# Top-10 indices of 8,192 rows: extraction of tile 60 moved behind the last sums, a fourth thin tile, constant matmuls in the last gather, and the rows of one batch on GpSimd

## The chip, the cores and the metric

The kernel runs on one core of one Trainium2 chip. The metric is the device time of one execution in microseconds (us). "Executions" below are single runs of the whole kernel. Every ratio given is the mean time of one kernel's runs over the mean of the kernel before's runs in the same rounds, so it is not quite the ratio of the medians quoted beside it; in the ratios of the experiments the first round, whose execution was profiled, is left out.

## The reference, cut to what matters

```python
# x: 8192 x 8192 float32, k = 10
indices = np.argpartition(x, -k, axis=1)[:, -k:]
values = np.take_along_axis(x, indices, axis=1)
sorted_idx = np.argsort(-values, axis=1)
return np.take_along_axis(indices, sorted_idx, axis=1)      # 8192 x 10 int64
```

For each row the kernel returns the positions of its ten largest values, in falling order.

## The kernel before

The 8,192 rows go through in 64 tiles of 128 rows, numbered 0 to 63. A tile passes through these stations:

1. **load**: the input arrives in chunks by DMA.
2. **weigh**: ScalarE writes exp(36(x - 4.7)) into one of three `e` buffers; TensorE sums groups of it ("sums", bf16 matmuls of 512 columns).
3. **choose**: VectorE finds the 12 groups with the largest sums and writes their index.
4. **gather**: GpSimd fetches those groups from the tile.
5. **spread**: VectorE (and GpSimd, for one half) multiplies by a mask.
6. **extract**: TensorE turns the masked groups into rows of candidates. E60 to E63 name the extractions of the last four tiles, 24 matmul records each.
7. **rank**: VectorE sorts out the ten best.
8. **finish**: per batch of tiles, one-hot steps, rows and a few matmuls make the output.

The last three tiles (`TAIL = 3`) have a "thin" layout, in which choosing is shorter. The part of the schedule that the change touches:

```python
epool = ctx.enter_context(tc.tile_pool(name="e", bufs=3))
...
    for t in range(last):                       # last = 63
        interleave(choose_steps(t), rank_steps(t - LAG) if t >= LAG else [])
        if t >= 1:
            spread(t - 1)
        gather(t)
        weigh(t + 1)
        if 1 <= t < last - 1:
            extract(t - 1)                      # so E60 is queued ahead of ...
        ...
    run(rank_steps(last - 3))
    run(choose_steps(last))
    spread(last - 1)
    gather(last)
    extract(last - 2)
    extract(last - 1)
    ...
    run(rank_steps(last - 2))
    steps = finish_steps(batch_of[last - 3])
    run(steps[:2])
    spread(last, G)
    run(steps[2:7])
    extract(last)
    run(steps[7:-2])
    run(rank_steps(last - 1))
    run(rank_steps(last))
    ...
```

In the loop's last turn (t = 62), `weigh(63)` comes ahead of `extract(61)`. In the turn before it, `extract(60)` follows `weigh(62)`. TensorE therefore has E60 in its queue ahead of the sums of tile 63, and E61 behind them.

Of the kernel before, what the change touches and what calls it, by code (L numbers as in the profile page):

```python
# [10 lines left out]
P = 128  # L11
N = 8192
BANK = 512
KMAX = 10
G = 12
TB = 8
# [3 lines left out]
FINITE = 1e37  # L20
BIG_NEG = -1e30
LAG = 3
TAIL = 3
PAD = 208



# [8 lines left out]
def kernel(  # L36
# [6 lines left out]
    nc = tc.nc  # L43
# [3 lines left out]
    ntiles = nrows // P  # L47

    fp32 = mybir.dt.float32
# [11 lines left out]
    wide, thin = Layout(8), Layout(16)  # L61
# [5 lines left out]

    pad = ctx.enter_context(tc.tile_pool(name="pad", bufs=1)).tile([P, PAD], fp32, name="pad")
    nc.vector.memset(pad[:, 0:1], 0.0)
# [8 lines left out]
    fpsum = ctx.enter_context(  # L78
        tc.tile_pool(name="fpsum", bufs=1, space=bass.MemoryType.PSUM)
    )  # L80

    last = ntiles - 1

    starts = list(range(0, ntiles - TB, TB)) + [ntiles - TB - 1, ntiles - TAIL]
    sizes = [b - a for a, b in zip(starts, starts[1:] + [ntiles])]
    batch_of = {t: b for b, t0 in enumerate(starts) for t in range(t0, t0 + sizes[b])}

# [3 lines left out]
    def layout(t):  # L91
        return thin if t >= ntiles - TAIL else wide

# [26 lines left out]
    nc.vector.memset(ones, 1.0)  # L120
    for lay, nsend in ((wide, TB), (thin, TAIL)):
        R, A, S = lay.R, lay.A, lay.S
# [105 lines left out]
    def extract(t):  # L228
        mk = masked.pop(t)
        gs[t] = gpsum.tile([P, G * thin.R], fp32, tag="g", name="g")  # L230
        R = layout(t).R
        for c in range(G):
            nc.tensor.matmul(gs[t][:, c * R:(c + 1) * R], lhsT=mk[:, c, :, :].rearrange("p a s -> p (a s)"),  # L233
                             rhs=layout(t).place, start=True, stop=True)

    def rank_steps(t):
        n = G * layout(t).R
        g = gs.pop(t)[:, 0:n]
        b = batch_of[t]
        pos = batch[b][1][:, t - starts[b], :]  # L240
        t8a = small.tile([P, 8], fp32, tag="t8a", name="t8a")
        t8b = small.tile([P, 8], fp32, tag="t8b", name="t8b")
        g2 = small.tile([P, G * thin.R], fp32, tag="g2", name="g2")[:, 0:n]
        return [
            lambda: nc.vector.max(out=t8a, in_=g),  # L245
            lambda: nc.vector.match_replace(out=g2, in_to_replace=t8a, in_values=g,  # L246
                                            imm_value=BIG_NEG),
            lambda: nc.vector.max_index(out=pos[:, 0:8], in_max=t8a, in_values=g),  # L248
            lambda: nc.vector.max(out=t8b, in_=g2),  # L249
            lambda: nc.vector.max_index(out=pos[:, 8:16], in_max=t8b, in_values=g2),  # L250
            lambda: nc.vector.tensor_copy(out=tall[:, t:t + 1],
                                          in_=t8b[:, KMAX - 9:KMAX - 8]),
        ]


    def finish_steps(b):
        cidb, posb = batch.pop(b)
        n = sizes[b]
        lay = layout(starts[b])
        R, A, S, W = lay.R, lay.A, lay.S, lay.W  # L260
        r0 = starts[b] * S
        out_rows = out_u32.rearrange("(r a) n -> r (a n)", a=A)

        queue = nc.sync if b >= len(starts) - 2 else nc.scalar
        slot = bpool.tile([P, TB, KMAX], u16, tag="slot", name="slot")[:, 0:n, :]
        low = bpool.tile([P, TB, KMAX], u16, tag="low", name="low")[:, 0:n, :]
        hot = bpool.tile([P, TB, KMAX, G], fp16, tag="hot", name="hot")[:, 0:n]
        pick = bpool.tile([P, TB, KMAX], fp32, tag="pick", name="pick")[:, 0:n, :]
        val = bpool.tile([P, TB, KMAX], fp32, tag="val", name="val")[:, 0:n, :]
        rows = bpool.tile([P, TB, wide.A, KMAX], fp32, tag="rows", name="rows")[:, 0:n, 0:A]  # L270
        if b == len(starts) - 1:
            fo = spsum.tile([P, wide.W], fp32, tag="s", name="fo")
        else:
            fo = fpsum.tile([P, wide.A * KMAX], fp32, tag="fo", name="fo")
        fo = fo[0:n * S, 0:A * KMAX]
        o = opacks[b % 2][0:n * S, 0:A]
        hshape = [P, n, KMAX, G]
        rshape = [P, n, A, KMAX]

        def move(i):  # L280
            nc.tensor.matmul(fo, lhsT=lay.send[:, i, 0:n * S],  # L281
                             rhs=rows[:, i].rearrange("p a k -> p (a k)"),
                             start=i == 0, stop=i == n - 1)

        return [
            lambda: nc.vector.tensor_scalar(
                out=slot, in0=posb[:, 0:n, 0:KMAX], scalar1=R.bit_length() - 1,
                scalar2=None, op0=ALU.logical_shift_right),
            lambda: nc.vector.tensor_scalar(
                out=low, in0=posb[:, 0:n, 0:KMAX], scalar1=R - 1,  # L290
                scalar2=None, op0=ALU.bitwise_and),
            lambda: nc.vector.tensor_tensor(
                out=hot, in0=slot.unsqueeze(3).to_broadcast(hshape),
                in1=slots.unsqueeze(1).unsqueeze(1).to_broadcast(hshape), op=ALU.is_equal),
            lambda: nc.vector.tensor_tensor(
                out=hot, in0=hot, in1=cidb[:, 0:n, 0:G].unsqueeze(2).to_broadcast(hshape),
                op=ALU.mult),
            lambda: nc.vector.reduce_sum(out=pick, in_=hot, axis=X_AX),  # L298
            lambda: nc.vector.scalar_tensor_tensor(
                out=val, in0=low, scalar=float(W), in1=pick, op0=ALU.mult, op1=ALU.add),  # L300
            lambda: nc.vector.tensor_tensor(  # L301
                out=rows, in0=val.unsqueeze(2).to_broadcast(rshape),
                in1=lay.own_a.unsqueeze(1).unsqueeze(3).to_broadcast(rshape), op=ALU.mult),
        ] + [lambda i=i: move(i) for i in range(n)] + [
            lambda: nc.vector.tensor_copy(
                out=o[:, :, :, 0], in_=fo.rearrange("p (a k) -> p a k", k=KMAX)),
            lambda: queue.dma_start(out=out_rows[r0:r0 + n * S, :],
                                        in_=o.rearrange("p a k two -> p (a k two)")),
        ]

    def interleave(*lists):
        for group_ in zip(*[l for l in lists if l]):
# [3 lines left out]
    def run(steps):  # L316
        for step in steps:
            step()
# [3 lines left out]
    with tc.manual_schedule():  # L322
        weigh(0)
        later = []
        for t in range(last):
            interleave(choose_steps(t), rank_steps(t - LAG) if t >= LAG else [])
            if t >= 1:
                spread(t - 1)
            gather(t)
            weigh(t + 1)  # L330
            if 1 <= t < last - 1:
                extract(t - 1)
            todo = {last - 5: 6, last - 4: TB, last - 3: TB}.get(t, 3)
            run(later[:todo])
            later = later[todo:]
            done = t - LAG
            if done >= 0 and batch_of[done] != batch_of[done + 1]:
                later += finish_steps(batch_of[done])
            if t + 3 < ntiles:
                load(t + 3)  # L340
        run(rank_steps(last - 3))
        run(choose_steps(last))
        spread(last - 1)
        gather(last)
        extract(last - 2)
        extract(last - 1)
        nc.vector.tensor_scalar(
            out=good[:, 0:nsums], in0=eall, scalar1=FINITE, scalar2=None, op0=ALU.is_lt,
        )
        run(rank_steps(last - 2))  # L350
        steps = finish_steps(batch_of[last - 3])
        run(steps[:2])
        spread(last, G)
        run(steps[2:7])
        extract(last)
        run(steps[7:-2])
        run(rank_steps(last - 1))
        run(rank_steps(last))


        nc.scalar.activation(out=e10, in_=tall, func=ACTF.Exp, bias=bias[:, 0:1], scale=BETA)
        final = finish_steps(batch_of[last])
        run(final[:-2])
        run(steps[-2:])
        run(final[-2:])
        nc.vector.scalar_tensor_tensor(
            out=good[:, nsums:nsums + ntiles], in0=e10, scalar=SLACK, in1=wall[:, :, G],
            op0=ALU.mult, op1=ALU.is_gt,
        )

    ngood1 = small.tile([P, 1], fp32, tag="ngood1")
    nc.vector.reduce_sum(out=ngood1, in_=good, axis=X_AX)
    gps = fpsum.tile([P, wide.A * KMAX], fp32, tag="fo", name="gps")[0:1, 0:1]
    nc.tensor.matmul(gps, lhsT=ngood1, rhs=ones, start=True, stop=True)
    ngood = consts.tile([1, 1], i32)
    nc.vector.tensor_copy(out=ngood, in_=gps)
# [56 lines left out]
```

## Time and profile before

| what | value |
|---|---|
| timed executions | 683.30, 683.42, 683.85 us |
| span of the profiled execution | 684.6 us |
| last chunk of input landed | 652.0 us |
| last sums end | 658.86 us |
| index of tile 63 written | 662.73 us |
| its gather ends | 667.96 us |
| ranking of tile 63 starts | 675.29 us |

The last five rows are times in the profiled execution, counted from its start. They form one chain: each row waits for the row above. Everything up to the landing is one long stage at the speed of the loads; the change works on the 32 us behind it. The lines themselves stand in the prediction.

### The profile page before, as it was taken

What the parts mean: (1) busy time and instruction counts of PE and PEld (TensorE: products, weight loads), DVE (VectorE), ACT (ScalarE), POOL (GpSimd) and SP (SyncE); (2) the same over time, 40 slices, a digit from 0 to 9 for tenths busy, and PEclk for the clock granted to TensorE, in tenths of its full rate; (3) what the DMA queues carried; (4) which work ended last, traced back from release to release, by engine and by line L of the source; (5) the groups of instructions that cost most, each with busy time, mean ns of one, the idle gap of its engine ahead of it and who ended that gap; (6) DMA issues with size and microseconds to landing.
All of it is one profiled execution on the core that took longest, in us unless ns stands there. A gap on an engine that the chain in (4) does not pass through costs nothing.

```text
span 684.6 us, 7943 instructions
## 1 busy us (share of the span) xinstructions
PE 550.9 (80%) x2645; PEld 345.7 (51%) x2690; DVE 554.9 (81%) x1335; ACT 488.8 (71%) x264; POOL 178.8 (26%) x134
## 2 busy tenths in 40 slices
PE   1588887888888898778887779888978779888786
PEld 0146653554544565545454356455545446656465
DVE  2568888889868987888887995898978798699567
ACT  4777777776877767877777777777777777777820
POOL 0113313313322322321332232232233133223310
PEclk9856788858876678787888885876789778779765
DMA  9999999999999999999999999999999999999800
GB/s 352 420 421 420 419 421 419 421 419 420 420 421 420 419 421 420 421 419 421 420 421 418 420 420 420 420 420 421 419 421 419 421 415 419 418 418 387 323 2 7
DMA packets 73696, 269.77 MB, mean 394 GB/s; under 512 B 4382, under 2 KB 5046, under 8 KB 73654
## 3 DMA queue, kind: packets, MB, share of 16 engines
q1 hardware_dynamic: 72960, 268.54, 96.1%
q10 hardware_dynamic: 694, 0.71, 0.4%
q8 instruction: 21, 0.34, 0.2%
q14 instruction: 21, 0.17, 0.1%
HBM read 268.58 MB, written 0.66 MB: 393 GB/s over the span
## 4 chain that ended last, share of the span: by engine, by line
DMA 63%; PE 8%; DVE 8%; SPq 6%; ACT 6%; issue 4%; POOL 3%; ACTq 0%; DVEq 0%
DMA xt<-in_x_dram 63%; PE s L169 7%; SPq L101 6%; ACT e L162 6%; POOL cand L203 3%; DVE wall L189 2%; PE g L233 1%; DVE m L190 1%; DVE masked L221 1%; DVE cidb L194 0%; DVE cidb L192 0%; DVE wall L193 0%; DVE rows L301 0%; DVE g L246 0%; DVE pick L298 0%
## 5 line engine op out<-in xcount | busy, mean ns | idle before, releaser
L162 ACT ACTIVATE e<-xt,bias 128x4096 bf16<-128x4096 f32 (+2 forms) x131 | 475.5, 3630 | 160.5 <-DMA xt<-in_x_dram 138.6
L169 PE MATMUL s<-e,group 128*128 128x512 bf16 x979 | 335.3, 498 | 123.9 <-ACT e L162 119.6
L169 PEld LDWEIGHTS <-group 128*128 128x128 bf16 x1024 | 122.3, 123 | 310.9 <-issue 255.3
L233 PEld LDWEIGHTS g<-cpack,masked 128*128 128x128 f32 x1536 | 212.2, 219 | 20.4 <-issue 9.0
L233 PE MATMUL g<-cpack,masked 128*128 128x8 f32 (+1 forms) x1536 | 203.7, 272 | 5.0 <-DVE masked L221 2.5
L203 POOL INDIRECT_COPY cand<-xt,idx 128x192 f32 x64 | 64.8, 1013 | 483.2 <-DMA xt<-in_x_dram 168.2
L189 DVE MAX8 wall<-s 128x8 f32<-128x1024 f32 (+1 forms) x64 | 77.2, 1207 | 119.3 <-PE s L169 113.1
L221 POOL TENSOR_TENSOR masked<-cand,cpack 128x768 f32<-128x768 f32 x63 | 113.1, 1795 | 5.2
L192 DVE FIND_INDEX8 cidb<-wall,s 128x8 uint16<-128x1024 f32 (+1 forms) x64 | 76.9, 1201 | 0.0
L194 DVE FIND_INDEX8 cidb<-wall,m 128x8 uint16<-128x1024 f32 (+1 forms) x64 | 76.7, 1198 | 0.0
L190 DVE MATCH_REPLACE8 m<-wall,s 128x1024 f32<-128x1024 f32 (+1 forms) x64 | 76.2, 1191 | 0.0
L193 DVE MAX8 wall<-m 128x8 f32<-128x1024 f32 (+1 forms) x64 | 75.9, 1186 | 0.0
L221 DVE TENSOR_TENSOR masked<-cand,cpack 128x768 f32<-128x768 f32 x64 | 62.0, 969 | 2.2 <-POOL cand L203 2.2
L281 PE MATMUL fo<-rows,send 128*64 128x160 f32 (+3 forms) x128 | 28.0, 370 | 1.1 <-DVE rows L301 1.1
L162 ACT ACTIVATION_READ_ACCUMULATOR e<-xt,bias 128x1 f32 x131 | 24.4, 186 | 0.0
L281 PEld LDWEIGHTS fo<-rows,send 128*64 128x64 f32 (+2 forms) x128 | 18.5, 162 | 3.5 <-DVE rows L301 1.7
L248 DVE FIND_INDEX8 posb<-t8a,g 128x8 uint16<-128x96 f32 (+1 forms) x64 | 16.9, 264 | 0.0
L250 DVE FIND_INDEX8 posb<-t8b,g 128x8 uint16<-128x96 f32 (+1 forms) x64 | 16.8, 263 | 0.0
L246 DVE MATCH_REPLACE8 g<-t8a,g 128x96 f32<-128x96 f32 (+1 forms) x64 | 16.3, 254 | 0.0
L245 DVE MAX8 t8a<-g 128x8 f32<-128x96 f32 (+1 forms) x64 | 16.2, 254 | 0.0
L249 DVE MAX8 t8b<-g 128x8 f32<-128x96 f32 (+1 forms) x64 | 16.1, 251 | 0.0
L195 DVE TENSOR_SCALAR idx<-cidb,cpack 128x12 uint16<-128x12 uint16 x64 | 14.1, 221 | 0.1
(37 smaller groups left out, 94.0 us busy)
## 6 DMA issues: line engine op xcount, KB each, us to landing
xt<-in_x_dram SPq DMA_DIRECT2D x248, 1024.0 KB, 16.3
xt<-in_x_dram SPq DMA_DIRECT2D x16, 512.0 KB, 9.8
out_dram<-opack ACTq DMA_DIRECT2D x6, 80.0 KB, 5.4
cpack<-topk_cpack ACTq DMA_DIRECT2D x1, 141.0 KB, 3.9
out_dram<-opack ACTq DMA_DIRECT2D x1, 70.0 KB
out_dram<-opack SPq DMA_DIRECT2D x1, 60.0 KB, 2.1
out_dram<-opack SPq DMA_DIRECT2D x1, 30.0 KB, 1.5
```

The costliest lines, as they stand in the source:

```text
L101: nc.sync.dma_start(out=dst[:, s:s + n, :], in_=src[:, s:s + n, :])
L162: nc.scalar.activation(out=e[:, 0:n * W], in_=xts[t][:, s0 * W:(s0 + n) * W], func=ACTF.Exp, bias=bias[:, 0:1], scale=BETA, accum_out=eall ...
L169: nc.tensor.matmul(ss[t][:, j:j + BANK], lhsT=lay.group[:, s0 + i, :], rhs=e[:, i * W + j:i * W + j + BANK], start=s0 + i == 0, stop=s0 + ...
L189: lambda: nc.vector.max(out=w16[:, 0:8], in_=m),
L190: lambda: nc.vector.match_replace(out=m2, in_to_replace=w16[:, 0:8], in_values=m, imm_value=-1.0),
L192: lambda: nc.vector.max_index(out=cid[:, 0:8], in_max=w16[:, 0:8], in_values=m),
L193: lambda: nc.vector.max(out=w16[:, 8:16], in_=m2),
L194: lambda: nc.vector.max_index(out=cid[:, 8:16], in_max=w16[:, 8:16], in_values=m2),
L203: nc.gpsimd.add_instruction(mybir.InstIndirectCopy(name=nc.get_next_instruction_name(), ins=[nc.gpsimd.lower_ap(xts[t]), nc.gpsimd.lower_a ...
L221: eng.tensor_tensor(out=masked[t][:, g0:g1], in0=cand[:, g0:g1].unsqueeze(2).to_broadcast(shape), in1=layout(t).own.rearrange("p (c s) -> ...
L233: nc.tensor.matmul(gs[t][:, c * R:(c + 1) * R], lhsT=mk[:, c, :, :].rearrange("p a s -> p (a s)"), rhs=layout(t).place, start=True, stop=True)
L281: nc.tensor.matmul(fo, lhsT=lay.send[:, i, 0:n * S], rhs=rows[:, i].rearrange("p a k -> p (a k)"), start=i == 0, stop=i == n - 1)
```

## The change

The intent is to take E60 out of the way of the last sums, to let the thin layout start one tile earlier, to keep TensorE's clock up for E63 by matmuls on constants, and to take work from VectorE. The core of the diff:

```diff
-TAIL = 3
+TAIL = 4
+WARM = 12
...
+        spreader = nc.gpsimd if b == len(starts) - 2 else nc.vector
...
-            lambda: nc.vector.tensor_tensor(
+            lambda: spreader.tensor_tensor(
                 out=rows, ...
...
+    def warm(n):
+        idle = fpsum.tile([P, BANK], fp32, tag="fo", name="idle")
+        for i in range(n):
+            nc.tensor.matmul(idle, lhsT=wide.group[:, 0, :],
+                             rhs=wide.group[:, 0:BANK // P, :].rearrange("p s m -> p (s m)"),
+                             start=True, stop=True)
...
-            if 1 <= t < last - 1:
+            if 1 <= t < last - 2:
                 extract(t - 1)
...
-        run(rank_steps(last - 3))
+        extract(last - 3)
+        extract(last - 2)
+        steps = finish_steps(batch_of[last - TAIL])
+        run(steps[:4])
         run(choose_steps(last))
         spread(last - 1)
         gather(last)
-        extract(last - 2)
         extract(last - 1)
+        run(rank_steps(last - 3))
+        run(rank_steps(last - 2))
...
-        run(rank_steps(last - 2))
-        steps = finish_steps(batch_of[last - 3])
-        run(steps[:2])
+        warm(WARM)
         spread(last, G)
-        run(steps[2:7])
         extract(last)
+        run(steps[4:7])
         run(steps[7:-2])
```

Left out here are the batch boundaries that follow from `TAIL`, a PSUM tile made one bank wide, and the padding.

More of the change, by code (lines that the diff above doesn't have):

```diff
@@ L22 @@
 LAG = 3
-TAIL = 3
-PAD = 208
+TAIL = 4
+WARM = 12
+PAD = 224
 class Layout:
@@ L82 @@
     last = ntiles - 1
-    starts = list(range(0, ntiles - TB, TB)) + [ntiles - TB - 1, ntiles - TAIL]
+    starts = list(range(0, ntiles - 2 * TB, TB)) + [ntiles - 2 * TB, ntiles - TB - 2, ntiles - TAIL]
     sizes = [b - a for a, b in zip(starts, starts[1:] + [ntiles])]
@@ L273, in finish_steps @@
         else:
-            fo = fpsum.tile([P, wide.A * KMAX], fp32, tag="fo", name="fo")
+            fo = fpsum.tile([P, BANK], fp32, tag="fo", name="fo")
         fo = fo[0:n * S, 0:A * KMAX]
+        spreader = nc.gpsimd if b == len(starts) - 2 else nc.vector
         o = opacks[b % 2][0:n * S, 0:A]
@@ L330 @@
             weigh(t + 1)
-            if 1 <= t < last - 1:
+            if 1 <= t < last - 2:
                 extract(t - 1)
-            todo = {last - 5: 6, last - 4: TB, last - 3: TB}.get(t, 3)
+            todo = {last - 6: 6, last - 5: TB, last - 4: TB}.get(t, 3)
             run(later[:todo])
@@ L336 @@
             done = t - LAG
-            if done >= 0 and batch_of[done] != batch_of[done + 1]:
+            if 0 <= done < last - TAIL and batch_of[done] != batch_of[done + 1]:
                 later += finish_steps(batch_of[done])
@@ L372 @@
     nc.vector.reduce_sum(out=ngood1, in_=good, axis=X_AX)
-    gps = fpsum.tile([P, wide.A * KMAX], fp32, tag="fo", name="gps")[0:1, 0:1]
+    gps = fpsum.tile([P, BANK], fp32, tag="fo", name="gps")[0:1, 0:1]
     nc.tensor.matmul(gps, lhsT=ngood1, rhs=ones, start=True, stop=True)
```

## The prediction

> **What bounds the kernel now.** I read the page first, then the chain of waits, then the timeline of the last 45 us, then the windows of the same stretch.
>
> The page's slices show one long stage and a short tail:
>
> ```profile
> DMA  9999999999999999999999999999999999999800
> GB/s 352 420 421 420 419 421 419 421 419 420 420 421 420 419 421 420 421 419 421 420 421 418 420 420 420 420 420 421 419 421 419 421 415 419 418 418 387 323 2 7
> ...
> DMA 63%; PE 8%; DVE 8%; SPq 6%; ACT 6%; issue 4%; POOL 3%; ACTq 0%; DVEq 0%
> ```
>
> The input (268.5 MB) streams at about 420 GB/s for 37 of 40 slices; nothing in the change touches that stage except the layout of one more tile. The last chunk of the last tile lands at 652.0 us by the trace's landings, and the span is 684.6 us. So some 32 us at the end run without loads, and that tail is what the change works on. Tiles are numbered 0 to 63; E60 to E63 are the extractions of the last four (24 matmuls each).
>
> ```profile
> 645.72 2.89 PE L169 MATMUL s<-e,group 128*128 128x512 bf16 x8 [2.17 <-ACT e L162]
> ...
> 648.40 5.13 PE L233 MATMUL g<-cpack,masked 128*128 128x8 f32 x24
> ...
> 655.34 1.15 ACT L162 ACTIVATE e<-xt,bias 128x1024 bf16<-128x1024 f32 x1 [3.68 <-issue]
> ...
> 656.98 1.15 ACT L162 ACTIVATE e<-xt,bias 128x1024 bf16<-128x1024 f32 x1 [0.40 <-ACT e L162]
> 657.36 1.02 POOL L203 INDIRECT_COPY cand<-xt,idx 128x192 f32 x1 [8.83 <-PE s L169]
> ...
> 658.70 2.75 PE L233 MATMUL g<-cpack,masked 128*128 128x16 f32 x24
> 658.90 0.70 DVE L189 MAX8 wall<-s 128x8 f32<-128x512 f32 x1 [3.56 <-PE s L169]
> ...
> 662.49 0.23 DVE L195 TENSOR_SCALAR idx<-cidb,cpack 128x12 uint16<-128x12 uint16 x1
> ...
> 663.73 5.27 PE L233 MATMUL g<-cpack,masked 128*128 128x16 f32 x24 [2.29 <-DVE good L347]
> ...
> 666.95 1.01 POOL L203 INDIRECT_COPY cand<-xt,idx 128x192 f32 x1 [6.94 <-issue]
> 668.00 1.76 DVE L221 TENSOR_TENSOR masked<-cand,cpack 128x1536 f32<-128x1536 f32 x1 [2.19 <-POOL cand L203]
> ...
> 669.90 5.27 PE L233 MATMUL g<-cpack,masked 128*128 128x16 f32 x24 [0.90 <-DVE masked L221]
> ```
>
> What to see. E60 (648.40, 5.13 us at half clock) stands ahead of the last tile's sums. The activation has only three e buffers, so its fourth piece waits 3.68 us for TensorE to give one back; the last sums end at 658.88 though their data landed at 652.0. From there a serial chain runs: choose (658.90 to 662.73), gather (to 667.96), mask (1.76), E63 (to 675.17), two rankings (the second begins at 675.38), finish.
>
> ```profile
> 658.70:661.50 2.80, 2.75 (x25) 2.65 (x23) 2.57 (x6) 0.00 (x0) 1.31 (x1) 1.00 0.00 0
> ...
> 663.70:669.00 5.30, 5.27 (x24) 5.19 (x24) 3.04 (x13) 0.00 (x0) 1.01 (x1) 0.50 0.00 0
> 669.00:670.00 1.00, 0.10 (x2) 0.13 (x1) 1.00 (x2) 0.00 (x0) 0.00 (x0) 0.50 0.00 0
> 670.00:675.00 5.00, 5.00 (x24) 5.00 (x24) 4.79 (x13) 0.00 (x0) 0.00 (x0) 0.50 0.01 3
> ```
>
> The third column from the right is the granted clock: an extraction takes 2.75 us at 1.00 and 5.27 at 0.50.
>
> **What the skill says.** The Trainium skill, "TensorE: Matmul & The Clock Gate", Part 1, has the clock halve after an idle window of about 3.4 us that runs free, and double after a busy one. The trace agrees: every change of the clock falls on one grid of 3.41 us. It also adds something: I counted matmuls per grid cell over the whole trace, and a cell leads to full clock when it holds about 6 or more of the 512-column matmuls; a cell with 24 extraction matmuls and at most three of those leads to half clock. Extractions do not count as work for the gate. The same page, Part 2, says matmuls stay in program order; the E60 wait above agrees. "GPSIMD Engine Reference", section 8, says that GpSimd shares SBUF interfaces with VectorE and suffers from instructions with two SBUF inputs. Agrees: from the end of the index to the end of the gather is 5.30 us in most tiles (one mask beside it), 6.25 to 6.70 where a one-hot, a product or a row spread runs beside it. "Perfetto Trace Analysis", on the GPSIMD lifecycle, warns that GpSimd spans are unreliable: the gather shows 1.0 us but costs 5.3, so I count from its index.
>
> **The change, part by part.**
>
> (1) Sums first. E60 leaves the path of the last sums. With no wait for e, the activation runs 645.6 + 3 x 2.0 + 2 x 1.25 = 654.1, and the last two sums end near 654.5. The fourth thin tile costs load time: thin chunks land 2.55 us apart, wide ones 2.49, so four chunks add about 0.3 us. Sums end near 654.8: 4.1 us earlier.
>
> (2) VectorE takes half of that back. Choosing tile 62 ends at 653.1 + 0.3, its companion mask at 654.3; then the first four steps of the previous batch (0.1 + 0.1 + 0.90 + 0.55, from the rows at 669.67 and 670.61 and the two shifts) end at 655.95. Choosing tile 63 starts there: 2.9 us earlier, index at 659.8.
>
> (3) GpSimd takes more. Those one-hot steps now run beside gather 62 and lengthen it by about 1.05: 653.4 + 6.35 = 659.8 (658.4 before). Then its half mask with VectorE beside it takes 1.8, to 661.6, and gather 63 behind it 4.65 (the first tile, with no mask beside it): 666.3 instead of 667.96. Gain 1.7. Mask 63 on VectorE ends at 668.1.
>
> (4) TensorE now has E60, E61 and E62 in a row after 654.8, and E62 waits for the mask at 661.7. The clock should drop one grid cell after the sums, so a part of E60 or E61 and all of E62 run cold: my count over the grid's phase gives E61 ending at 661.4 to 664.2, E62 at 667 to 669. The 12 constant matmuls (0.427 each cold, 0.216 warm) take 4 to 5 us and end at 671 to 674, E63 then 2.75 us. Mean end 675.4, against 675.17 now. If E62 ends early enough for the constants to lie inside the gather, E63 runs 668.1 to 670.9 instead, and the second ranking starts at 671.2, set by VectorE.
>
> (5) The spread on GpSimd: 960 elements at 1.55/768 us each, about 1.95 us instead of 1.16, but it leaves VectorE and is needed only by matmuls after E63. VectorE saves 1.16, no longer the limit in the slow branch.
>
> (6) The last batch has four tiles: its five VectorE steps grow from 2.41 to about 2.8 us, its matmuls from 6 to 8 (0.175 each, +0.35). Loss 0.7.
>
> (7) Earlier, the batch's cast falls in tile 58 right behind its own matmuls, so VectorE stalls some 4 us there and load 63 is issued near 635 instead of 631.4. The load queue then still holds nearly all of tile 62 (its chunks land until 641.8), so I expect no gap. Tiles 60 and 61 are thin or late enough to absorb it.
>
> **Sum.** Fast branch: ranking 63 starts at 671.2 (-4.2), last batch +0.7: span 681.1, time about 679.9 (timed runs lie 1.2 below the profiled span). Slow branch: start at 675.4, +0.7: span 685.4, time 684.2.
>
> **Rivals.** *TensorE becomes the bound* (the slow branch): for it, all four extractions come after the sums, and the gate ignores extractions, so 12 more matmuls delay E63 by 4 us to save 2.5. Against it: a count of twelve looks as if it was fitted to a gap that was measured. Time 684.2. *The gather chain stays the bound* (the fast branch): for it, each link is a plain latency of the trace; against it, it needs E62 to end by about 665. Time 679.9. *The load stream suffers*: a late load 63 starves the queue, sums end 1 to 3 us later and all gains go: 684 to 687; against it the queue's depth. *A full gain*: the 4.1 us of the sums arrive whole at the end and the warm clock adds 2.5: 677.5; against it parts (2) and (3).
>
> **Range.** I put 45% on the fast branch and 55% on the slow one: 0.45 x 679.9 + 0.55 x 684.2 = 682.3. Rounded up for the load risk: 682.5. The range covers both branches and half of the other two: 679.0 to 686.0. Two per cent is 13.7 us, more than the whole gain of any branch: faster 0.02, same 0.97, slower 0.01.
>
> **What would show it.** Right: activation of the last tile without the 3.68 us wait; last sums near 655; choice of tile 63 starting near 656 behind the one-hot; gather 63 ending near 666; granted clock 1.00 in E63 (2.75 us). The branch shows in whether E63 waits for its mask (fast) or for the constants (slow). Wrong if the last chunk lands later than 653, if the clock holds through E60 to E62, or if the spread on GpSimd holds back matmuls.

## The result, and the profile after

The changed kernel took **686.85 us** in the median of four executions (684.34, 686.77, 686.92, 686.92). Four executions of the kernel before in the same rounds took 682.85 to 683.85, median 683.36. The ratio is 1.0042, with a 95% interval of 1.0018 to 1.0066. So the change made the kernel 0.4% slower. That is within 2%, as predicted, but the time lies above the predicted range, while the span of the profiled execution, 685.1 us, is only 0.5 us longer than the profiled span before.

The chain that ended last, by engine and by line, in the page of the kernel after:

```profile
DMA 59%; PE 14%; DVE 9%; SPq 6%; ACT 5%; issue 4%; POOL 3%; ACTq 0%; POOLq 0%; DVEq 0%
DMA xt<-in_x_dram 58%; PE s L170 8%; SPq L102 6%; ACT e L163 5%; PE g L234 5%; POOL cand L204 3%; DVE wall L190 2%; DVE m L191 1%; DVE cidb L195 1%; DVE cidb L193 1%; DMA out_dram<-opack 1%; DVE wall L194 1%; PE idle L317 1%; DVE masked L222 1%; PE fo L283 0%
```

PE rose from 8% to 14%. The extractions (`g L234`) went from 1% to 5%, and the constants (`idle L317`) are themselves on the chain. This says that TensorE now sets the end. The timeline of the last stretch shows how (start, duration, engine, line, operation, tiles, count, idle time before it and its releaser):

```profile
652.30 1.14 ACT L163 ACTIVATE e<-xt,bias 128x1024 bf16<-128x1024 f32 x1
...
653.44 1.13 ACT L163 ACTIVATE e<-xt,bias 128x1024 bf16<-128x1024 f32 x1
...
655.14 12.50 PE L234 MATMUL g<-cpack,masked 128*128 128x16 f32 x72
...
655.49 0.91 DVE L294 TENSOR_TENSOR hot<-slot,slots 128x720 f16<-128x720 uint16 x1
656.43 0.53 DVE L297 TENSOR_TENSOR hot<-hot,cidb 128x720 f16<-128x720 f16 x1
...
659.71 1.01 POOL L204 INDIRECT_COPY cand<-xt,idx 128x192 f32 x1 [6.09 <-DVE wall L194]
...
660.81 2.31 POOL L222 TENSOR_TENSOR masked<-cand,cpack 128x768 f32<-128x768 f32 x1
...
667.48 4.94 PE L317 MATMUL idle<-group 128*128 128x512 bf16 x12
667.68 1.76 DVE L222 TENSOR_TENSOR masked<-cand,cpack 128x1536 f32<-128x1536 f32 x1 [2.13 <-POOL cand L204]
...
672.26 2.75 PE L234 MATMUL g<-cpack,masked 128*128 128x16 f32 x24
...
675.05 0.37 DVE L246 MAX8 t8a<-g 128x8 f32<-128x192 f32 x1 [2.69 <-PE g L234]
```

ScalarE's last two pieces no longer wait for a buffer. The sums end at about 655.3, 3.6 us earlier than in the profiled execution before. But then E60, E61 and E62 run as one block of 72 matmuls without a gap, 12.50 us, and the 12 constants start only when that block is over. They end after the mask of tile 63, which is finished at 669.4; E63 waits 2.8 us more, until 672.26. The ranking of tile 63 starts at 675.05, against 675.29 before: the whole gain at the sums is spent on TensorE. GpSimd shows a second delay: its half mask begins only at 660.81, when the index of tile 63 is just written (660.75), so the last gather waits until 663.12 for GpSimd. Here it costs nothing, as E63 waits for the constants, 2.8 us longer than for its mask.

The windows of the kernel after (stretch, length, then busy us and count of PE, PEld, DVE, ACT and POOL, then the granted clock, the DMA share and GB/s):

```profile
655.30:658.50 3.20, 3.20 (x31) 3.20 (x30) 3.13 (x10) 0.00 (x0) 0.00 (x0) 0.97 0.00 0
658.50:662.00 3.50, 3.50 (x18) 3.50 (x18) 3.42 (x7) 0.00 (x0) 2.20 (x2) 0.50 0.00 0
662.00:665.50 3.50, 3.50 (x18) 3.50 (x18) 3.37 (x18) 0.00 (x0) 1.12 (x1) 0.50 0.02 5
```

TensorE is busy in every microsecond of these rows, and yet the clock falls to half at 658.3 and stays there. That was argued in the prediction, and it came. The prediction took its rule from a count of 512-column matmuls in cells of 3.41 us. Recounted over the whole trace of the kernel before, cells in which seven or more of them start were followed by the full clock in 66 of 67 cases, and cells with three or fewer by the half clock in 55 of 56; with four to six it went either way (35 full, 37 half).

All this is what the prediction called the slow branch, to some tenths of a microsecond. Why was the time still outside the range? The answer lies in the other kernel. The profiled execution of the kernel before had itself taken 686.37 us, not 683.42; its record says so. In every run the time is the span plus 1.8 us (684.6 and 686.37; 685.1 and 686.92; 681.4 and 683.20). So the trace before, with its 3.68 us wait, shows an execution about 3 us slower than the three timed ones. The kernel before has executions of more than one kind.

How common they are came out beside the experiments, where the kernel before was executed 62 more times: 20 of those took over 685 us (up to 687.6), the rest 682.1 to 684.7.

### The profile page after: what moved, and what is told of

Its sections match the earlier page's. It is cut to its first block, busy times and chain, and to the rows that moved or that the text cites. A ratio compares the mean times of both kernels' runs of the same rounds, so it can differ in the third digit from the quotient of the medians. Undisturbed runs are those within 1.5% of the kernel's fastest.

```text
span 685.1 us, 8017 instructions
## 1 busy us (share of the span) xinstructions
PE 561.8 (82%) x2702; PEld 341.5 (50%) x2702; DVE 552.0 (81%) x1335; ACT 488.8 (71%) x264; POOL 182.3 (27%) x135
## 4 chain that ended last, share of the span: by engine, by line
DMA 59%; PE 14%; DVE 9%; SPq 6%; ACT 5%; issue 4%; POOL 3%; ACTq 0%; POOLq 0%; DVEq 0%
DMA xt<-in_x_dram 58%; PE s L170 8%; SPq L102 6%; ACT e L163 5%; PE g L234 5%; POOL cand L204 3%; DVE wall L190 2%; DVE m L191 1%; DVE cidb L195 1%; DVE cidb L193 1%; DMA out_dram<-opack 1%; DVE wall L194 1%; PE idle L317 1%; DVE masked L222 1%; PE fo L283 0%
## 5 line engine op out<-in xcount | busy, mean ns | idle before, releaser
L170 PE MATMUL s<-e,group 128*128 128x512 bf16 x1024 | 349.7, 506 | 112.3 <-ACT e L163 112.1
L170 PEld LDWEIGHTS <-group 128*128 128x128 bf16 x1024 | 124.4, 125 | 312.0 <-issue 261.9
L234 PEld LDWEIGHTS g<-cpack,masked 128*128 128x128 f32 x1536 | 205.0, 213 | 20.9 <-DVE masked L222 7.7
L234 PE MATMUL g<-cpack,masked 128*128 128x8 f32 (+1 forms) x1536 | 197.2, 268 | 5.3 <-DVE masked L222 5.3
L222 POOL TENSOR_TENSOR masked<-cand,cpack 128x768 f32<-128x768 f32 x63 | 114.6, 1818 | 5.2
L283 PE MATMUL fo<-rows,send 128*64 128x160 f32 (+2 forms) x128 | 26.6, 357 | 1.9 <-DVE rows L303 1.9
L283 PEld LDWEIGHTS fo<-rows,send 128*64 128x64 f32 (+1 forms) x128 | 17.5, 155 | 4.0 <-DVE rows L303 2.5
```

Source lines behind the costliest of these rows:

```text
L170: nc.tensor.matmul(ss[t][:, j:j + BANK], lhsT=lay.group[:, s0 + i, :], rhs=e[:, i * W + j:i * W + j + BANK], start=s0 + i == 0, stop=s0 + ...
L222: eng.tensor_tensor(out=masked[t][:, g0:g1], in0=cand[:, g0:g1].unsqueeze(2).to_broadcast(shape), in1=layout(t).own.rearrange("p (c s) -> ...
L234: nc.tensor.matmul(gs[t][:, c * R:(c + 1) * R], lhsT=mk[:, c, :, :].rearrange("p a s -> p (a s)"), rhs=layout(t).place, start=True, stop=True)
L283: nc.tensor.matmul(fo, lhsT=lay.send[:, i, 0:n * S], rhs=rows[:, i].rearrange("p a k -> p (a k)"), start=i == 0, stop=i == n - 1)
```

## The experiments

The gather instruction itself could not be used in experiments. All experiments therefore replace the gather by a **stand-in** on GpSimd that takes about as long, and compare kernels that all have it. Their output is wrong; the check at the end was set so that the fallback does not run (`passed < 1` for `passed < checks`). Names beginning with s, p and q are the first, second and third stand-in.

### Getting a fair stand-in

The first stand-in was one long addition on GpSimd:

```diff
-        nc.gpsimd.add_instruction(mybir.InstIndirectCopy(...))
+        head = xts[t][:, 0:1984]
+        nc.gpsimd.tensor_tensor(out=head, in0=head,
+            in1=idxs[t][:, 0:1].bitcast(bf16).to_broadcast([P, 1984]), op=ALU.add)
+        nc.gpsimd.tensor_copy(out=cands[t].rearrange("p g s -> p (g s)"), in_=xts[t][:, 0:192])
```

It ran under the kernel before, the kernel after, the kernel after without constants (`WARM = 0`), and the kernel after with `run(steps[:4])` moved from ahead of the last choice to behind the rankings of tiles 60 and 61 ("late").

> The kernel before, with the gather replaced by a stand-in on GpSimd (an addition of 1984 elements over the same tile, waiting for the same index, then a copy of 192 elements into the same candidates; the result is wrong on purpose, and the fallback at the end is switched off). It calibrates the stand-in: from the index to the end of the stand-in should be 5.3 us with one mask beside it (4.5 to 6.0 will do), and its time should lie within 3 us of the original's 683.4. Theory A (phase of the clock's grid): the trace of the kernel before was an unlucky draw, its E60 ran cold (5.13 us) and its sums ended at 658.9; in most runs E60 runs warm (2.75 us) and the sums end at 655 to 656, which is why timed runs are 3 us shorter than the traced one. This look then has E60 near 2.75 us and sums before 657.5, unless it is unlucky too. Rival B (the trace is typical in its tail and the timed runs gain elsewhere): E60 is cold again and the sums end near 658.9.

> The changed kernel with the same stand-in. If the stand-in stands for the gather, the ratio to the stand-in of before repeats the measured 1.004 (+2 to +4 us; timed against the true kernel before it shows the same plus the stand-in's own offset). Both theories: E60, E61, E62 in one run of matmuls after the sums, then 12 constant matmuls, then E63 late, near 672.

> The changed kernel with the stand-in and no constant matmuls. Theory T (TensorE's queue is the bound, the constants delay E63): E63 starts as soon as its mask is there (668 to 669), runs cold (5.2 us), ends near 673.5, and the time falls by 1 to 2 us against the changed kernel. Rival (the constants pay, as they were meant to): the time rises by 1 to 2.5 us, as E63 is cold and not otherwise earlier.

> The changed kernel with the stand-in, and the four steps of the previous batch not before the last choice but after the rankings of tiles 60 and 61, in the shadow of the last gather. Theory T: choice of tile 63 starts 1.6 us earlier and gather 62 is 1 us shorter, gather 63 ends about 1 us earlier, but E63 still waits for the constants, so the time stays within 0.5 us of the changed kernel. Rival (the gather chain is the bound): the time falls by about 1.1 us.

Measured, with five rounds: 685.62 (ratio 1.0027), 693.69 (1.0157), 692.75 (1.0124) and 686.93 us (1.0050). These sizes are not those of the real kernels, and the trace of s_after says why; first two lines of GpSimd, then one of VectorE:

```profile
656.35 4.14 POOL L206 TENSOR_TENSOR xt<-xt,idx 128x1984 f32<-128x1984 f32 x1 [0.16 <-DVE tall L253]
660.55 0.34 POOL L210 COPY cand<-xt 128x192 f32<-128x192 f32 x1
```

```profile
657.06 3.47 DVE L289 TENSOR_SCALAR slot<-posb 128x60 uint16<-128x60 uint16 x1
```

In the kernel after this VectorE step takes 0.19 us. Here it ends at 660.53, when the long GpSimd instruction ends. The stand-in holds VectorE up, which the true gather does not do to this step. The pair s_after and s_after_late shows only that steps of VectorE beside a long GpSimd instruction can cost 6.8 us; for the kernel it was discarded.

The second stand-in is one short addition that waits for the index, and 19 short copies:

```diff
+        flat = cands[t].rearrange("p g s -> p (g s)")
+        nc.gpsimd.tensor_tensor(out=flat[:, 0:G], in0=xts[t][:, 0:G],
+                                in1=idxs[t].bitcast(bf16), op=ALU.add)
+        cuts = [G + (16 * G - G) * i // PIECES for i in range(PIECES + 1)]     # PIECES = 19
+        for a, b in zip(cuts, cuts[1:]):
+            nc.gpsimd.tensor_copy(out=flat[:, a:b], in_=xts[t][:, a:b])
```

> The kernel before with a second stand-in for the gather: twenty short GpSimd instructions (an addition that waits for the index, then nineteen copies of 9 or 10 elements) instead of one long one, as the long one held VectorE up by 3 to 4 us at a time, which the gather never does. Calibration: index to end of the stand-in near 5.3 us, no VectorE instruction stretched by more than 0.5 us, time within 1 us of the true kernel before (683.4 or, in the other group of its executions, 686.4).

> The changed kernel with the second stand-in. If it is a fair stand-in, its time is 2 to 4 us over that of the kernel before with the same stand-in, as with the true gather (+3.5), E61 and E62 run cold behind the sums, the twelve constant matmuls follow E62 and E63 starts near 672.

Measured: 682.90 (ratio 0.9980) and 686.95 us (1.0040). It nearly reproduces the true difference (4.0 us here, 3.5 there), though it took only 3.46 us where the gather takes 5.30. The kernel after took nearly the same time with a gather 1.8 us shorter (686.95 against 686.85, in other rounds), so the gather does not seem to set its end.

The third stand-in has `PIECES = 33` and takes 5.2 us. It is used in all that follows.

### The two kernels, without constants, and with the clock held up earlier

> The kernel before with the stand-in lengthened to 33 copies, which makes it 5.3 us from the index to its end with one mask beside it, as the gather's (with 19 copies it was 3.46). Calibration: time within 0.7 us of the true kernel before, with the same two groups of executions (near 683.4 and near 686.2).

> The changed kernel with the lengthened stand-in: 686 to 687.5, ratio to the true kernel before 1.004 to 1.006; tail as in the changed kernel's own trace: sums end near 654.7, E62 ends near 667.5, constants to 672, E63 2.75 us.

> The same without the twelve constant matmuls. Theory T (TensorE's queue sets the end of the tail, the constants wait behind E62 and delay E63): E63 starts when its mask is there (about 669) and not at 672, runs cold (5.2 us), ends 0.5 to 1.5 us earlier, and the time falls by 0.5 to 2 us. Rival (the constants pay for themselves): the time rises by 1 to 2.5 us.

The fourth run adds six constant matmuls to the kernel *before*, between the two halves of the sums of tile 62, so that the clock is full when E60 starts:

```diff
             s0 += n
+            if t == last - 1 and h == 0:
+                warm(6)
```

> The kernel before with the stand-in and six constant matmuls in TensorE's idle stretch between the two halves of tile 62's sums, nothing else moved. Theory A (the kernel before has a fast and a slow group because the clock at the second half of tile 62, E60 and the last sums depends on where the 3.41 us grid falls): with the clock held at full there, the slow group goes, all executions lie below 684.5, the median is 681.5 to 683.2, and in the trace E60 takes about 2.75 us and the last sums end before 656.5. Rival B (the two groups come from elsewhere): two groups 3 us apart stay, median within 0.5 us of the stand-in kernel before.

| run | median us (executions) | ratio, 95% interval | ranking 63 starts in the trace |
|---|---|---|---|
| q_before | 684.11 (683.14 to 687.89) | 1.0009 [0.9987, 1.0031] | 672.49 |
| q_after | 687.68 (686.71 to 688.01) | 1.0047 [1.0034, 1.0060] | 675.32 |
| q_after_warm0 | 686.13 (684.89 to 688.43) | 1.0033 [1.0013, 1.0052] | 673.78 |
| q_before_prewarm | 683.42 (683.25 to 685.22) | 0.9992 [0.9977, 1.0006] | 672.66 |

The stand-in now gives both kernels' times to within 0.9 us (684.15 for the kernel before in the same rounds, 686.85 for the kernel after above). The profiled execution of q_before was one of the quick ones (683.20), so its trace shows what the trace of the true kernel before does not. Its TensorE and ScalarE:

```profile
648.25 2.74 PE L233 MATMUL g<-cpack,masked 128*128 128x8 f32 x24
...
650.39 2.00 ACT L163 ACTIVATE e<-xt,bias 128x2048 bf16<-128x2048 f32 x1
...
650.85 5.30 PE L170 MATMUL s<-e,group 128*128 128x512 bf16 x16
...
652.39 1.13 ACT L163 ACTIVATE e<-xt,bias 128x1024 bf16<-128x1024 f32 x1
...
655.99 2.75 PE L233 MATMUL g<-cpack,masked 128*128 128x16 f32 x24
...
661.01 5.27 PE L233 MATMUL g<-cpack,masked 128*128 128x16 f32 x24 [2.28 <-DVE good L347]
...
667.10 5.27 PE L233 MATMUL g<-cpack,masked 128*128 128x16 f32 x24 [0.81 <-DVE masked L221]
```

E60 takes 2.74 us, at the full clock, and ScalarE waits for no buffer. In this execution the wait that the change was made to remove isn't there. The sums end at about 656.15, only 0.9 us later than in the kernel after. E61, E62 and E63 have idle time between them, so TensorE's queue doesn't set the end: E63 starts when its mask is there. Against this execution, and not against the slow one, the change has to win.

The constants cost 1.5 us in the traces (start of ranking 63 in q_after against q_after_warm0), although E63 with them takes 2.75 us. The medians differ by as much, but the intervals of the two ratios overlap, and three executions of q_after_warm0 took over 687 us; so the timings alone don't settle this cost. Without the constants the kernel's median is still some 2 us above that of q_before.

The six constants ahead of E60 left one of six executions above 685, where q_before had two; the others lie within 0.3 us. This points to the clock at E60 and the sums before it as what parts the executions, but six executions are too few to show it.

### Each moved part by itself

Here the first part alone goes into the kernel before ("sums"), and the same part is undone in the kernel after ("e60back"), with and without constants:

```diff
 # q_before_sums, on the kernel before
-            if 1 <= t < last - 1:
+            if 1 <= t < last - 2:
...
-        run(rank_steps(last - 3))
+        extract(last - 3)
         run(choose_steps(last))
...
+        run(rank_steps(last - 3))
         run(rank_steps(last - 2))
```

```diff
 # q_after_e60back, on the kernel after (q_after_e60back_warm0: WARM = 0 as well)
-            if 1 <= t < last - 2:
+            if 1 <= t < last - 1:
...
-        extract(last - 3)
         extract(last - 2)
```

> The kernel before on the stand-in of 33 copies, with the first part of the change alone: the extraction of tile 60 goes behind the last sums and its ranking behind the last gather (no constants, three thin tiles, no mask rows on GpSimd). Theory A, the clock makes the groups of executions: the sums no longer wait behind a slow extraction, so the spread shrinks and the sums end near 655.2. Theory B, three extractions behind the sums make TensorE the bound: 61 waits for 60 and 62 for 61 at the half clock (5.2 us each), extraction 63 starts 1 to 2 us later than in q_before (667.1) if 62 ends behind its mask, and the time is 684 to 686. If instead the part is a gain, the sums end 0.9 earlier and the time is 682 to 683. A result within 0.5 of q_before says that the part alone is neutral.

> The changed kernel on the stand-in, with the extraction of tile 60 put back ahead of the last sums and all else kept (four thin tiles, 12 constants, rows on GpSimd). If what is lost is the work of TensorE behind the sums, 2.7 us (one extraction at the full clock) leave it: extraction 63 starts near 669.8 in place of 672.5 and the time is about 685 against 687.7 for q_after. If the thin tiles or the moved rows are what costs, it stays within 1 us of q_after.

> As q_after_e60back, and without the constants. By the theory of TensorE as the bound nothing of the loss is left: 682.5 to 684, as q_before (about 683.5). If the four thin tiles cost by themselves, it stays above q_before by 1 us or more. Against q_after_warm0 (686.1) it isolates the extraction moved behind the sums without the constants.

| run | executions, us | median | ranking 63 starts in the trace |
|---|---|---|---|
| kernel before, same rounds | 682.60 to 683.76 (4), 684.72, 685.44 to 686.82 (6) | 685.44 | |
| q_before_sums | 684.40, 684.69, 684.75, 684.81, 685.07, 685.35 | 684.78 | 673.26 |
| q_after_e60back | 684.36, 684.46, 684.48, 686.20, 686.40, 687.57 | 685.34 | 673.17 |
| q_after_e60back_warm0 | 684.63, 684.68, 685.49, 686.17, 687.49, 687.84 | 685.83 | 674.83 |

In these rounds the kernel before fell into its slow kind more often than not (in the rounds of the first stand-in, on the same chip, in 3 of 11). That makes q_before_sums the clearest run. All its six executions lie within 1 us, between the two kinds of the kernel before: the slow kind is gone and so is the quick one. On the average it is neither faster nor slower (ratio 1.0000 [0.9977, 1.0022]). Its TensorE shows what bounds the profiled one:

```profile
655.26 17.97 PE L233 MATMUL g<-cpack,masked 128*128 128x8 f32 x96
673.16 3.44 PE L281 MATMUL fo<-rows,send 128*48 128x160 f32 x12
```

All four extractions run in one block of 96 matmuls, 17.97 us without a gap. Behind the sums, TensorE is now the bound. That this holds in the five other executions too would explain their even times, but they were not traced. Its windows, columns as before:

```profile
655.30:658.50 3.20, 3.20 (x29) 3.20 (x28) 2.97 (x8) 0.00 (x0) 3.12 (x24) 0.93 0.00 0
658.50:662.00 3.50, 3.50 (x19) 3.50 (x18) 3.40 (x13) 0.00 (x0) 3.39 (x13) 0.50 0.01 2
...
665.50:669.00 3.50, 3.50 (x18) 3.50 (x18) 3.43 (x4) 0.00 (x0) 0.00 (x0) 0.50 0.02 5
669.00:673.00 4.00, 4.00 (x20) 4.00 (x20) 3.29 (x12) 0.00 (x0) 0.00 (x0) 0.50 0.00 0
```

Almost fifteen microseconds of nothing but extractions, and the clock stays at half. E60 takes the stretch at the full clock that E61 had in q_before, so that E61 runs at the half clock too: behind the sums E60 costs as much as a half-clock extraction. Ahead of the sums, in the quick trace, it fills idle time of TensorE.

The undo agrees: with E60 back, the median of the kernel after is 2.3 us lower (687.68 to 685.34, in two calls; ratios 1.0047 [1.0034, 1.0060] and 1.0012 [0.9986, 1.0038]) and ranking 63 starts 2.1 us earlier. Its times spread out again, too. Without the constants in both kernels the same undo is worth only 0.3 us of the median (686.13 to 685.83; ratios 1.0033 and 1.0016, intervals overlapping). So the gain stands clear of the noise, and only just, where the constants are there to be held up; for E60 alone it is not shown. With E60 back, taking the constants away as well brought nothing more (1.0016 [0.9989, 1.0043]). That miss is worth a note. TensorE's last part, first in q_after_e60back, then in q_after_e60back_warm0:

```profile
661.84 4.80 PE L234 MATMUL g<-cpack,masked 128*128 128x16 f32 x24 [2.28 <-DVE masked L222]
666.48 4.07 PE L317 MATMUL idle<-group 128*128 128x512 bf16 x12
670.39 2.75 PE L234 MATMUL g<-cpack,masked 128*128 128x16 f32 x24
```

```profile
669.52 5.27 PE L234 MATMUL g<-cpack,masked 128*128 128x16 f32 x24 [2.30 <-DVE masked L222]
```

With E60 ahead of the sums, E62 ends at 666.6, so the constants end only some 1.2 us behind the mask of tile 63, and E63 then runs 2.5 us shorter than at the half clock: in these traces they pay for themselves. What they cost in q_after is owed to the block in front of them. The second of these executions took 686.17 us, yet in it E60 had the full clock (2.75 us) and ScalarE waited for no buffer. So in this kernel a time above 685 is not by itself the mark of a slow E60.

My expectation that nothing would be left of the loss was wrong too. The quick executions stay at 684.4 to 684.7, about 1 us above those of the kernel before in the same rounds (682.60 to 683.76). GpSimd shows part of this; q_before first, then q_after_e60back (copies of the last two stand-ins, with the half mask of tile 62 between them):

```profile
653.82 4.24 POOL L210 COPY cand<-xt 128x5 f32<-128x5 f32 x33
658.13 1.54 POOL L221 TENSOR_TENSOR masked<-cand,cpack 128x768 f32<-128x768 f32 x1
660.09 0.84 POOL L205 TENSOR_TENSOR cand<-xt,idx 128x12 f32<-128x12 f32 x1 [0.41 <-DVE idx L196]
```

```profile
655.43 5.34 POOL L211 COPY cand<-xt 128x5 f32<-128x5 f32 x33
660.86 2.24 POOL L222 TENSOR_TENSOR masked<-cand,cpack 128x768 f32<-128x768 f32 x1
663.06 0.21 POOL L206 TENSOR_TENSOR cand<-xt,idx 128x12 f32<-128x12 f32 x1
```

In q_before GpSimd waits for the last index. In the changed kernel the one-hot steps run beside the stand-in of tile 62 (5.34 us for 4.24) and a VectorE mask beside the half mask (2.24 for 1.54), so the index, written at 660.8, waits 2.2 us for GpSimd.

### The third part undone

The last run takes the four one-hot steps away from there too, so that of the change little more than the thin tile and the rows on GpSimd is left (ranking 60 stays behind the last gather, and the one-hot steps now come ahead of the last mask, not behind it); q_before was repeated beside it.

```diff
 # q_after_undo3, on q_after_e60back_warm0
-        run(steps[:4])
         run(choose_steps(last))
...
         nc.vector.tensor_scalar(out=good[:, 0:nsums], ...)
+        run(steps[:4])
         warm(WARM)
         spread(last, G)
```

> The kernel before on the stand-in once more, beside the next kernel on the same chip: two groups as before, 682.6 to 684 and 685 to 687, gather 63's stand-in starts within 0.5 us of its index.

> The changed kernel on the stand-in with three parts undone: extraction 60 ahead of the sums, no constants, and the four one-hot steps behind the rankings 60 and 61 (no longer beside the gather of tile 62 and ahead of choosing 63); the four thin tiles and the rows on GpSimd stay. If the one-hot steps beside the gather of 62 are the rest of the loss, its stand-in takes about 5.2 us in place of 6.2, GpSimd is free when index 63 comes (q_after_e60back: 2.3 us late), and the fast group is at 683 to 683.5, as that of q_before_again. If the thin tiles cost by themselves, it stays at 684.5.

Measured: q_before_again 684.87 us (683.68 to 687.78), q_after_undo3 685.60 (684.83 to 686.52), ratios 1.0013 and 1.0018. GpSimd was on time again (the last stand-in starts 0.1 us behind its index), as expected. But the one-hot steps now lie beside the last stand-in, which took 5.8 us in place of 5.1, and no execution came under 684.8. So in this trace the moved steps are not the rest of the loss; their place only chooses which gather is slowed down. What remains is seen in the traces. From the start of ranking 63 to the end of the span it is 8.91 us in q_before (672.49 to 681.4) and 9.53 in q_after_undo3 (673.47 to 683.0). That 0.6 us is the last batch with four tiles in place of three (its VectorE steps from the first shift to the rows take 2.9 us in place of 2.4, as in the two true kernels). The intervals of these two runs overlap, so of the timings alone nothing about the rest is settled.

### Looking for a version that beats both

First, constants only where TensorE idles in the trace of q_before, the ranking of tile 62 ahead of the last mask, and the rows on GpSimd:

```diff
 # q_best, on the kernel before
         extract(last - 2)
+        warm(10)
         extract(last - 1)
+        warm(14)
...
         run(steps[:2])
+        run(rank_steps(last - 1))
         spread(last, G)
...
-        run(rank_steps(last - 1))
         run(rank_steps(last))
```

> The kernel before on the stand-in, with constants only where TensorE idles by its trace (10 between extractions 61 and 62, 14 behind 62), ranking 62 ahead of the last mask, and the rows of the batch that ends with tile 60 on GpSimd. By theory the gate counts the constants: extraction 62 runs at 2.75 us at 661.0 and 63 at 2.75 in place of 5.27, ranking 63 starts at 669.9 in place of 672.5, and the time is 680 to 681.5, under q_before by 2 to 3 us. If the constants don't open the clock in time it is 682 to 683, from the ranking alone; if they hold extraction 62 up, slower than q_before.

Second, E60 in quarters, put where TensorE waits for ScalarE, alone and with such constants:

```diff
 # q_split, on the kernel before (q_split_best: also warm(12), warm(10) and the ranking as in q_best)
+            if t == last - 1:
+                extract(last - 3, 0, 3)
             weigh(t + 1)
...
             s0 += n                               # in weigh
+            if t == last and h < 3:
+                extract(last - 3, CUTS[h], CUTS[h + 1])      # CUTS = [3, 6, 9, 12]
```

> The kernel before on the stand-in, with the extraction of tile 60 in four quarters on TensorE: one ahead of the first part of the last sums and one behind each of the first three parts, in the stretches in which TensorE waits for ScalarE (1.9, 1.0, 1.0 us in the trace of q_before_sums). If theory A holds (the slow executions come from extraction 60 at the half clock, which holds up the last sums and the buffers of ScalarE), the group at 685.4 to 686.8 goes away without TensorE becoming the bound behind the sums: all executions at 682.5 to 684, no wait for a buffer on ScalarE, the sums end by 656.5. If the slow executions have another source they remain.

> As q_split, with 12 constants between extractions 61 and 62 and 10 behind 62, and ranking 62 ahead of the last mask. Extractions 62 and 63 at 2.75 us, ranking 63 starts 3.8 us behind the end of mask 63 in place of 5.6 (q_before): 680.5 to 682.5. If the constants end behind the mask of 62 or 63, as 14 of them did in q_best, it is no faster than q_split.

Measured: q_best 684.98 us (682.18 to 687.08; ratio 0.9990 [0.9964, 1.0016]), q_split 684.79 (682.82 to 687.76; 1.0017 [0.9984, 1.0050]), q_split_best 684.45 (682.30 to 685.02; 0.9993 [0.9964, 1.0022]). None beats the kernel before. The profiled execution of q_best was a slow one (687.08). In it the last 14 constants took 4.87 us, at the half clock, and ended 1.1 us behind the mask of tile 63 (672.8 against 671.7), so they held E63 up. And it shows the slow kind once more:

```profile
649.86 5.12 PE L233 MATMUL g<-cpack,masked 128*128 128x8 f32 x24
...
654.84 5.54 PE L170 MATMUL s<-e,group 128*128 128x512 bf16 x16
...
656.79 1.15 ACT L163 ACTIVATE e<-xt,bias 128x1024 bf16<-128x1024 f32 x1 [4.37 <-issue]
```

The long E60 and the wait for a buffer come together here, as in the true kernel before; in q_before and q_before_sums both are absent. But a long E60 is not needed for a wait. The trace of q_before_again, the same kernel as q_before (684.64 us), lies between:

```profile
646.43 3.41 PE L170 MATMUL s<-e,group 128*128 128x512 bf16 x8 [1.53 <-ACT e L163]
...
649.68 2.74 PE L233 MATMUL g<-cpack,masked 128*128 128x8 f32 x24
...
653.59 1.15 ACT L163 ACTIVATE e<-xt,bias 128x1024 bf16<-128x1024 f32 x1 [1.23 <-issue]
```

E60 has the full clock, but the eight sums of tile 62 ahead of it took 3.41 us in place of 1.89 (q_before), and ScalarE waited 1.23 us. In p_before the same three figures are 3.57, 3.03 and 1.41 us. So the clock at the sums of tile 62 counts as well as that at E60, and there are steps between the two kinds. In q_split two executions at 687.4 and 687.8 remained. I had expected none. Their traces were not taken, so what else makes executions slow stays open. In the trace of q_split the last choice started 0.5 us later than in q_before. The quarters were not the cause: VectorE was busy without a break from the choice for tile 62 on, and that had started 1.6 us later than in q_before, behind sums of tile 62 at the half clock (3.57 us). The index of tile 63 came at 661.3 in place of 660.0 (its own instruction took 1.06 us in place of 0.23).

## Why the prediction was wrong

By its own steps (in short: the conversion of the traced span to a time failed, and behind it the choice of the execution that the gain was counted from):

- **(1) Sums first: right in the trace, wrong in its worth.** The sums ended at 655.3 (said: 654.8), and the 3.68 us wait was gone. But "4.1 us earlier" was counted against the profiled execution. In the quick execution of q_before the sums end at 656.15 without any change. There the step is worth 0.9 us, and two thirds of the 62 executions are of the quicker kind (some of these may, like q_before_again, still hold a shorter wait).
- **(2) VectorE takes half back: right in kind.** Choosing started at 656.88 (said: 655.95), behind the one-hot steps, as told. The 0.9 us come from the choice for tile 62, which waited 2.4 us for its sums and wrote its index at 654.4 (said: 653.4).
- **(3) GpSimd takes more: right in kind, the half mask mis-sized.** Gather 62 ended at 660.73 (said: 659.8, the 0.9 us being those of step 2). The half mask took 2.31 us and not 1.8. The last gather ended at 667.64, not 666.3.
- **(4) TensorE: the slow branch, right to 0.3 us.** E62 ended at 667.6 (said: 667 to 669), the constants at 672.4 (671 to 674), ranking 63 started at 675.05 (675.4).
- **(5) and (6) right.** The rows took 1.98 us on GpSimd (said: 1.95) and held nothing up. The last batch grew by 0.6 to 0.7 us: from ranking 63 to the end of the span, 10.05 us against 9.31 in the two profiled executions.
- **(7) right.** No gap in the loads; the last chunk landed at 652.1.
- **Small readings.** The second ranking begins at 675.29 (said: 675.38), the last sums end at 658.86 (said: 658.88), and gathers with steps of a batch beside them took 5.88 to 6.70 us (said: 6.25 to 6.70). None of this moves the result.
- **The sum failed, in two terms.** First, "timed runs lie 1.2 below the profiled span" is false. It compared the median of three executions with the span of a fourth, slower one. Time is span plus 1.8 us. The slow branch's span of 685.4 (685.1 measured) thus means 687.2 us and not 684.2. With that one term corrected, the branch would have been 0.35 us from the result. None of the prediction's three signs of being wrong appeared: the loads ended at 652.1, the clock fell, and the rows held nothing up. It was wrong in the baseline, which it didn't name as a risk. Second, the weights: "45% on the fast branch" was a guess. E60 to E62 ran as one block up to 667.6 in the profiled execution, and in q_before_sums E60 to E63 did. The median comes from the slow branch, as far as the traces show. One execution of the changed kernel took 684.34; what was different in it is not known.

What the runs put in place of the sum: on the third stand-in, moving E60 behind the sums sends one more extraction into the half clock, and TensorE then sets the end in the trace; undone in the kernel after with its constants, it gives back 2.3 us. The constants cost 1.5 us by the traces, but only while E60 is in front of them, so the two figures are not to be added. The four-tile batch costs 0.6 us by the traces. The trade is also one of evenness: q_before_sums gives up executions at 683 to be rid of those at 686. That the slow kind of the kernel before comes from the half clock at the sums of tile 62 and at E60 is what its traces agree with; it is not proved for every execution.

The Trainium skill, "TensorE: Matmul & The Clock Gate", Part 1, says that the window of the clock gate runs free and that the same kernel therefore measures different counts of slow matmuls from run to run. This agrees with what was seen: the matmuls ahead of E60 are the same in the kernel before and in q_before, and E60 took 5.13 us in the one trace and 2.74 in the other; in two traces of one kernel, q_before and q_before_again, the second half of the sums of tile 62 took 1.89 and 3.41 us. I had read this and used it for the kernel after, and not for the kernel before.

## What to carry to other kernels

Before a wait in a profile is priced, compare the time of the profiled execution with the median of the timed ones. If it is slower by as much as the wait is long, the wait may be of that execution and not of the kernel. Work that fills an engine's idle time can be nearly free, as E60 was in the quick trace. Moved behind the last thing that the engine waits for, it can make that engine the bound, and warming up an engine is worth something only where it would otherwise be idle.

## What the Trainium skill lacked or had wrong

- "TensorE: Matmul & The Clock Gate", Part 1: it has the full clock granted after a busy window of about 3.4 us and says that this is a matter of time and not of a number of matmuls. In q_before_sums TensorE was busy with extractions (float32, 16 columns or fewer) for 17.97 us without a gap, and the granted clock was 0.50 from 658.5 to 673. Which kinds of matmul count for the gate the page says for transposes alone; the 512-column bf16 constants did bring the clock back (E63 in 2.75 us behind 12 of them).
- No page that I read says that the profiled execution can be slower than the median one, of the same kernel, by as much as the wait that is to be priced: here 686.37 us against 683.42.
